# Another order of all steps in a two-layer backbone kernel

## The chip, the cores and the metric

The kernel runs on one core of a Trainium2 chip. The core has five engines that run side by side, each on its own instruction stream: TensorE (PE, matrix products), VectorE (DVE), ScalarE (ACT), GpSimd (POOL) and SyncE (SP), which here issues most of the transfers. The metric is the device time of one execution in microseconds (us); the time of a kernel is the median of its runs. All times below are of the kernel before.

## The reference

A backbone of two layers works on 512 latent tokens of width 1024 and 256 context tokens, all in float32. Each layer has a token mixer and a SwiGLU feed-forward network (FFN, hidden width 2816). Both sit between normalisations whose shift, scale and gate come from a conditioning vector c (called adaLN rows here). Cut to what matters:

```
mod = silu(c) @ ada_w[i] + ada_b[i]            # six rows of 1024: shift, scale, gate, twice
h = rmsnorm(x, norm_g[i, 0]) * (1 + sc) + sh
y = mixer_i(h)                                 # layer 0: windowed attention, layer 1: chunked gMLP
x = x + g * rmsnorm(y, norm_g[i, 1])
f = (silu(h2 @ w_gate) * (h2 @ w_up)) @ w_out  # h2: the same normalisation again, FFN
x = x + g2 * rmsnorm(f, norm_g[i, 3])

gMLP: u, v = split(gelu(h @ w_in + b_in)); v = layernorm(v)
      y = (u * (w_s @ v + b_s)) @ w_o          # w_s mixes the 128 positions of a chunk
```

Layer 0's attention has 16 query heads and 4 key heads, a window of 128 tokens on either side, the context tokens as further keys, and a learned sink logit for each head. Only the latent tokens are an output, and layer 1 does not read the context, so its stream ends as keys and values of layer 0.

## The kernel before, in words

**Arithmetic.** A float32 product is made of three TensorE products: each operand is split into a high part (`high`, line 412, a cast on ACT) and a low part (`low`, line 419, a subtraction on DVE or POOL), and high·high, high·low and low·high are summed in PSUM. The weights are split in the kernel, so all weight data passes through ACT and DVE once before TensorE uses it.

**Weight stream.** The weights come in 88 units of 128x2048 (1 MB). `fetch` issues the transfer of a unit into one of two buffers called `w_raw`; the transfer of unit n waits until the last reader of unit n-2 is done. The split halves are `w_hi` and `w_lo`, four buffers each. A second class of small weights, the `ada_k` chunks of 128x1024, comes through the same SP queue.

**adaLN rows (class Ada).** A row of the second kind is made without TensorE for most of its way: `start` clears an accumulator `acc` on POOL (line 564), eight steps `add_chunk` (line 581, DVE) each add one chunk `ada_k` times a column of silu(c), `fold` (line 595) issues from POOL a transfer that adds the upper 64 partitions of `acc` to the lower ones, `mirror` issues from SP the transfer of the result back to the upper half, `stack` splits it into `acc_st` (ACT line 412, then DVE line 419 on 64 partitions), `total` (line 608) sums it over the partitions on TensorE into `ada_ps`, and `done` (lines 617 to 621) makes the `row`. The names of these steps begin with m and the row's number: m2 is layer 1's third row in its part of the string with "#2" at the end.

**Stages.** In order of time: start and keys/values (0 to 60 us), queries and attention (60 to 230), output projection and the norms behind it (230 to 290), the first FFN's input products (290 to 500), its output product `seven` (500 to 590), norms, the turn and the first part of the gMLP's v (590 to 640), the rest of v, u and the mixing (640 to 700), the gMLP's output product (700 to 755), heads of the second FFN (755 to 790), second FFN to the end (790 to 1108).

**The FFN.** Each of its weight units (22 a layer, numbered n here) is multiplied by a scheme of seven half-size products instead of eight. `diff` (line 1595) makes the sums and differences `T` of quarters of `w_raw`, on DVE (on POOL for the first four units); `part_low` for the first quarter makes `x` (line 419); `product` (line 1635) runs 12 matmuls of 128x256 into a PSUM tile `f`; `keep` (line 1642, ACT), `up2` (line 1646), `up1` (line 1650) and `gate1` (line 1654, all three DVE) combine the products, `silu` and `gates` (line 1665, DVE) end the unit.

**gMLP.** `v_part` (through `mm_a`, line 479) is 12 matmuls of 128x512, `u_part` (lines 2052 to 2054) 24. `vtmp` (line 2020) and `mu` (lines 2028, 2029) belong to the layer norm of v. Behind it, `st` is the split of u times the mixed v (line 2076 makes the factor `uT`), and `work` (line 479) the output product into `y`.

**What sets the order.** All of the work is cut into 3317 steps, each of which issues one or a few instructions on one engine. The program lists the steps with `at(time, step, args)` (line 785), which builds a name from the step and its arguments; the string `ORDER` (lines 41 to 395) holds all names, and a name's place in it is its rank. `run_plan` (line 795) issues the steps by rank:

```
count, rank = {}, {k: i for i, k in enumerate(ORDER)}
...
def run_plan():
    for _, _, key, step, args in sorted(plan, key=lambda e: e[:2]):
        step(*args)
```

No scheduler moves them afterwards. Each engine therefore runs its own instructions in the order of the string, and an instruction whose input is late holds up all that stands behind it on that engine, even if that could run. The same holds for the transfers in the SP queue.

Of the kernel before, what the change touches and what calls it, by code (L numbers as in the profile page):

```python
# [41 lines left out]
warm_0 rope_in x_fetch_5 square_in_5 rstd_in_5 norm_in_5_0 warm_1 norm_in_5_1 warm_2 warm_3 x_fetch_3 square_in_3  # L42
rstd_in_3 norm_in_3_1 dma rope_turn_0 rope_turn_1 x_fetch_4 norm_in_3_0 square_in_4 rstd_in_4 norm_in_4_0 norm_in_4_1
x_fetch_0 turn_in_3_1 x_fetch_1 turn_in_3_0 square_in_0 rstd_in_0 square_in_1 rstd_in_1 turn_in_5_1 turned_in_5_1
norm_in_0_1 warm_4 x_fetch_2 rope_turned_1 square_in_2 norm_in_0_0 turned_in_3_1 turn_in_4_1 rstd_in_2 turn_in_4_0
norm_in_1_0 norm_in_1_1 norm_in_2_0 turned_in_3_0 wfetch_0_0 turn_in_0_0 whigh_0_0 turned_in_0_0 turn_in_0_1
ada0_fetch_0 dma#2 turned_in_4_0 turn_in_5_0 ada0_fetch_1 turned_in_5_0 turn_in_1_0 turned_in_1_0 norm_in_2_1 <lambda>
ada0_rows_0 ada0_rows_out_0 ada0_fetch_2 wlow_0_0 wfetch_0_1 turn_in_2_1 ada0_cols_0 ada0_done_0 modulate0_ctx_0
turn_in_1_1 turn_in_2_0 ada0_rows_1 turned_in_2_0 ada0_fetch_3 modulated_ctx_0 kv_0_5 ada0_rows_out_1 modulate0_0
turned_in_1_1 modulated_high_0 ada0_fetch_4 turned_in_4_1 ada0_cols_1 ada0_done_1 rope_turned_0 kv_0_4 ada0_rows_2 dma#3  # L50
modulated_high_1 modulated_low_0 kv_0_0 modulate0_1 wfetch_1 kv_0_1 ada0_fetch_5 modulate0_ctx_1 m2start ada0_rows_out_2
ada0_cols_2 modulated_low_1 kv_1_0 kv_0_2 kv_1_2 whigh_0_1 wlow_0_1 modulated_ctx_1 ada0_done_2 modulate0_ctx_2 kv_1_1
kv_1_5 ada0_fetch_7 turned_in_2_1 modulated_ctx_2 modulated_high_2 modulate0_2 ada0_rows_3 m2fetch_0 ada0_rows_out_3
ada0_rows_4 ada0_fetch_6 wfetch_2 modulated_low_2 kv_2_2 ada0_cols_3 whigh_1_0 turned_in_0_1 ada0_done_3 modulate0_3
wlow_1_0 kv_0_3 modulated_high_3 kv_1_3 ada0_rows_out_4 modulate0_ctx_3 kv_2_5 m2fetch_1 modulated_low_3 modulated_ctx_3
kv_1_4 ada0_cols_4 ada0_done_4 modulate0_ctx_4 whigh_1_1 kv_2_4 modulated_ctx_4 m2add_0 kv_2_1 kv_3_5 modulated_high_4
ada0_rows_5 ada0_rows_out_5 ada0_rows_7 ada0_rows_out_7 kv_3_4 kv_2_3 kv_2_0 kv_3_0 m2add_1 ada0_cols_5 ada0_done_5
kv_3_2 modulate0_ctx_5 wlow_1_1 modulate0_4 modulated_low_4 dma#4 modulated_high_5 kv_4_5 m2fetch_2 kv_3_3
modulated_ctx_5 modulate0_5 modulated_low_5 kv_4_4 whigh_2_0 ada0_cols_7 ada0_done_7 m2add_2 m2add_3 kv_3_1 kv_4_1
m2fetch_3 ada0_rows_6 ada0_rows_out_6 kv_4_0 kv_5_0 kv_5_1 ada0_cols_6 wlow_2_0 q_first_0_0 whigh_2_1 wlow_2_1 kv_5_4  # L60
q_first_0_1 q_first_0_2 q_first_0_3 kv_4_3 kv_5_3 ada0_done_6 modulated_high_6 modulate0_6 modulated_low_6 kv_6_1 kv_6_0
kv_6_3 modulate0_ctx_6 kv_5_5 modulated_ctx_6 modulate0_7 modulated_high_7 modulated_low_7 kv_7_1 m2add_4 <lambda>#2
kv_7_0 q_first_0_4 q_first_0_5 kv_4_2 kv_5_2 kv_6_2 kv_7_2 kv_7_3 modulate0_ctx_7 modulated_ctx_7 q_first_0_6
q_first_0_7 m2add_5 m2add_6 m2add_7 kv_6_4 kv_7_4 kv_6_5 kv_7_5 wfetch_3 q_first_1_0 q_first_1_1 q_first_1_2 q_first_1_3
table_Exp k_copy_2_0 q_first_1_4 q_first_1_5 v_copy_3 k_copy_2_1 k_rope_2 v_copy_1 v_copy_0 q_first_1_6 k_copy_0_0
k_copy_0_1 k_rope_0 k_add_0 q_rows_0 whigh_3_0 v_copy_2 wlow_3_0_512_1024 whigh_3_1 wlow_3_1_512_1024 q_first_1_7
q_swap_0 k_copy_4_0 k_copy_4_1 wlow_3_0_0_512 k_turn_4_1 k_turn_0_1 k_add_2 wlow_3_1_0_512 q_cos_0 k_turn_0_0 k_turn_2_1
q_rows_1 q_sin_0 q_add_0 k_split_0_1 q_high_0_0 q_low_0_0 q_swap_1 v_copy_4 q_sin_1 k_split_0_0 k_turn_2_0 k_split_2_0
q_cos_1 k_split_4_1 k_turn_4_0 k_split_2_1 q_add_1 v_copy_5 k_split_4_0 q_high_0_1 q_low_0_1 q_high_1_0 q_high_1_1
q_low_1_1 q_low_1_0 wfetch_4 q_step_2_0 q_step_2_1 q_step_2_2 q_step_2_3 q_step_2_4 q_step_2_5 q_step_2_6 q_step_2_7  # L70
m2fold block_0 score_0_0 q_rows_2 score_0_1 bound_0_0 bound_0_1 q_step_3_0 whigh_4_0 wlow_4_0_512_1024 q_step_3_1
q_step_3_2 exp_0_0 m4fetch_0 q_swap_2 q_step_3_3 score_0_3 bound_0_3 score_0_2 bound_0_2 wlow_4_0_0_512 q_cos_2 exp_0_1
q_sin_2 whigh_4_1 exp_0_2 m4start q_step_3_4 q_step_3_5 exp_0_3 sink_0 q_add_2 q_step_3_6 q_step_3_7 q_rows_3
wlow_4_1_0_512 wlow_4_1_512_1024 total_0 normalise_0_0 normalise_0_2 block_1 block_2 block_3 block_4 score_1_0 q_swap_3
score_1_1 bound_1_0 normalise_0_3 q_high_2_0 q_step_4_0 bound_1_1 exp_1_0 exp_1_1 q_low_2_0 m2mirror q_step_4_1
q_step_4_2 score_1_2 m4fetch_1 score_1_3 bound_1_2 exp_1_2 normalise_0_1 bound_1_3 sink_1 m4add_0 q_step_4_3 exp_1_3
q_step_4_4 q_step_4_5 m2fetch_gain total_1 m4add_1 turn_0_0 turn_0_1 turned_0_0 normalise_1_1 m2stack normalise_1_2
score_2_1 bound_2_1 score_2_2 turn_0_2 q_step_4_6 bound_2_2 q_step_4_7 turned_0_2 turn_0_3 block_5 score_2_3 block_6
normalise_1_0 m2total_0_bank_t turned_0_1 score_2_0 turned_0_3 value_0 bound_2_3 exp_2_1 q_step_5_0 score_3_0 exp_2_2
q_rows_4 exp_2_3 normalise_1_3 turn_1_1 turn_1_4 bound_2_0 exp_2_0 sink_2 q_sin_3 block_8 m2done_0 q_step_5_1 score_3_2  # L80
block_7 turned_1_4 m4add_2 bound_3_0 turn_1_0 exp_3_0 turned_1_0 turned_1_1 score_3_1 q_swap_4 total_2 normalise_2_0
q_high_2_1 store_0 normalise_2_1 q_cos_3 turn_1_2 bound_3_2 exp_3_2 turn_1_3 bound_3_1 wfetch_5 q_step_5_2 exp_3_1
q_add_3 q_high_3_0 q_step_5_3 normalise_2_2 normalise_2_3 turned_1_2 turned_1_3 q_cos_4 score_4_0 bound_4_0 q_step_5_4
# [2150 lines left out]
```

## Time and profile before

| what | value |
|---|---|
| runs of the kernel | 1106.84, 1107.83, 1116.1 us; median 1107.83 |
| the profiled execution | 1109.65 us, of which the span from first to last instruction is 1107.9 us |
| busy time in the span | PE 1083.6 us (98%), DVE 941.2 (85%), ACT 602.5 (54%), POOL 264.1 (24%) |
| PE idle in the span | 24.3 us |
| mean granted TensorE clock | 0.995 |
| data moved | 181.25 MB, mean 164 GB/s |

The profile follows one execution. For each engine it gives the busy time by the line of the kernel that issued the instruction and by its operands (`f<-H,w_hi` is a product into `f` from `H` and `w_hi`). A list of waits says for an engine what the instruction that ended an idle time had waited for; the chain of work goes back from a late instruction to what released it, step by step; a table by windows gives busy times, the granted clock (PEclk) and the transfers for stretches of the span. A row of the timeline with `[2.14 <-DMA w_raw<-in_w]` stands for an instruction before which its engine was idle for 2.14 us, until that transfer had landed.

### The profile page before, as it was taken

The numbers are of one execution on the slowest core, as the hardware profiler recorded it, in microseconds if no ns is written. First come the engines' busy times: TensorE is split into PE (matmuls) and PEld (weight loads), VectorE is DVE, ScalarE is ACT, GpSimd is POOL, SyncE is SP. The second block draws the span as 40 slices with busy tenths as digits, with TensorE's granted clock in tenths as the row PEclk, the third lists the DMA queues.
The fourth block names the chain that finished last, engine by engine and source line by source line (L and its number), as shares of the span: only waits on it lengthen the run. The fifth ranks groups of instructions, "written<-read, shape, count | busy, mean of one in ns | idle before, by whom it ended". The sixth has DMA issues, their size and how long they took to land.

```text
span 1107.9 us, 17798 instructions
## 1 busy us (share of the span) xinstructions
PE 1083.6 (98%) x6894; PEld 950.1 (86%) x6894; DVE 941.2 (85%) x1382; ACT 602.5 (54%) x1055; POOL 264.1 (24%) x268
## 2 busy tenths in 40 slices
PE   9999999999999999999999998999999999999997
PEld 5787777778999999998888886878899999998886
DVE  6789998848998999998988687888998888879885
ACT  6356778656544545555665423436555545546662
POOL 2427777526400000002313211006300000003301
PEclk9999999999999999999999998999999999999999
DMA  9745441263255354669943576472143343369821
GB/s 360 280 155 170 144 130 46 80 198 142 77 194 196 128 187 161 195 216 280 219 72 113 196 233 233 137 248 77 38 160 129 131 153 124 125 223 320 165 34 76
DMA packets 50392, 181.25 MB, mean 164 GB/s; under 512 B 5370, under 2 KB 9722, under 8 KB 39172
## 3 DMA queue, kind: packets, MB, share of 16 engines
q1 hardware_dynamic: 42756, 165.44, 43.1%
q0 software_dynamic: 7552, 14.68, 7.7%
q8 instruction: 54, 0.88, 0.3%
q14 instruction: 30, 0.25, 0.1%
HBM read 171.71 MB, written 2.10 MB: 157 GB/s over the span
## 4 chain that ended last, share of the span: by engine, by line
PE 76%; DMA 10%; DVE 8%; issue 3%; ACT 2%; POOL 1%; SPq 1%; DVEq 0%; POOLq 0%; ACTq 0%
PE f L1635 31%; PE y L1819 13%; PE y L479 6%; PE y L1846 6%; DMA w_raw<-in_w 3%; DMA ada_k<-in_ada 2%; PE s_ps L1099 2%; PE pT_ps L1132 2%; PE o_ps L1148 2%; DMA ada_raw<-in_ada 2%; PE q_ps L861 1%; PE v L479 1%; PE fa L473 1%; DVE acc L581 1%; PE fa L471 1%
## 5 line engine op out<-in xcount | busy, mean ns | idle before, releaser
L1635 PE MATMUL f<-H,w_hi 128*128 128x256 f32 x960 | 177.4, 283 | 2.1 <-DVE fc L1646 2.1
L1635 PEld LDWEIGHTS f<-H,w_hi 128*128 128x128 f32 x960 | 149.9, 192 | 2.8 <-DVE fc L1646 2.5
L1635 PE MATMUL f<-H,w_lo 128*128 128x256 f32 x480 | 135.8, 283 | 0.0
L412 ACT CAST w_hi<-w_raw 128x1024 fp32r<-128x1024 f32 x90 | 94.3, 1052 | 60.0 <-DMA w_raw<-in_w 17.0
L1819 PE MATMUL y<-w_hi,s 128*128 128x512 f32 x448 | 120.1, 389 | 0.0
L1635 PE MATMUL f<-S,w_hi 128*128 128x256 f32 x640 | 118.1, 283 | 0.0
L412 ACT CAST w_hi<-T 128x1024 fp32r<-128x1024 f32 x80 | 83.4, 1048 | 58.2 <-PE f L1635 31.7
L1635 PEld LDWEIGHTS f<-S,w_hi 128*128 128x128 f32 x640 | 99.8, 192 | 0.5 <-ACT fc L1642 0.4
L419 DVE TENSOR_TENSOR w_lo<-T,w_hi 128x1024 fp32r<-128x1024 f32 x80 | 97.1, 1217 | 3.5 <-ACT w_hi L412 3.5
L1819 PEld LDWEIGHTS y<-w_hi,s 128*128 128x128 f32 x448 | 84.1, 188 | 17.5
L419 DVE TENSOR_TENSOR w_lo<-w_raw,w_hi 128x1024 fp32r<-128x1024 f32 (+1 forms) x81 | 95.4, 1183 | 4.2 <-ACT w_hi L412 4.2
L595 POOL DMA_DIRECT2D acc<-acc x8 | 6.9, 859 | 366.8 <-DVE acc L581 348.5
L1642 ACT COPY fc<-f 128x256 f32<-128x256 f32 x120 | 44.0, 373 | 92.0 <-PE f L1635 86.8
L1635 PEld LDWEIGHTS f<-H,w_lo 128*128 128x128 f32 x480 | 92.1, 192 | 0.0
L1635 PE MATMUL f<-S,w_lo 128*128 128x256 f32 x320 | 90.7, 283 | 0.0
L581 DVE SCALAR_TENSOR_TENSOR acc<-ada_k,sc,acc 128x1024 f32<-128x1024 f32 x56 | 71.6, 1279 | 13.3 <-DMA ada_k<-in_ada 13.0
L1807 POOL DMA_DIRECT2D t<-in_w x48 | 42.3, 944 | 169.1 <-DMA t<-in_w 95.4
L1819 PE MATMUL y<-w_lo,s 128*128 128x512 f32 x224 | 69.1, 390 | 0.4 <-DVE w_lo L419 0.4
L1635 PE MATMUL f<-H,x 128*128 128x256 f32 x480 | 65.1, 284 | 1.9 <-DVE x L419 1.8
L1126 POOL TENSOR_SCALAR p<-p,st 128x512 f32<-128x512 f32 (+1 forms) x64 | 57.1, 907 | 31.2 <-DVE st L1122 21.8
L1635 PEld LDWEIGHTS f<-H,x 128*128 128x128 f32 x480 | 60.7, 192 | 2.6 <-DVE x L419 2.5
L1110 ACT ACTIVATE p<-s_ps,st 128x512 f32<-128x512 f32 (+1 forms) x64 | 47.3, 740 | 26.4 <-DVE st L1105 24.6
(261 smaller groups left out, 2767.7 us busy)
## 6 DMA issues: line engine op xcount, KB each, us to landing
w_raw<-in_w SPq DMA_DIRECT2D x67, 1024.0 KB, 5.1
ada_k<-in_ada SPq DMA_DIRECT2D x56, 512.0 KB, 6.4
ada_raw<-in_ada SPq DMA_DIRECT2D x12, 1024.0 KB, 5.3
w<-in_w SPq DMA_DIRECT2D x12, 1024.0 KB, 7.0
t<-in_w POOLq DMA_DIRECT2D x48, 256.0 KB, 6.1
ada<-in_ada SPq DMA_DIRECT2D x8, 1024.0 KB, 10.9
t<-in_w SPq DMA_DIRECT2D x8, 1024.0 KB, 14.1
w_raw<-in_w SPq DMA_DIRECT2D x10, 512.0 KB, 5.4
```

Of the source, the lines that this page charges most:

```text
L412: nc.scalar.copy(out=hi, in_=src)
L419: (eng or nc.vector).tensor_tensor(out=v(lo), in0=v(src), in1=v(hi).bitcast(F32), op=ALU.subtract)
L479: nc.tensor.matmul(dst, l, w[:, n * 512:(n + 1) * 512], start=first and i == 0, stop=last and i == 2)
L581: nc.vector.scalar_tensor_tensor(out=self.acc, in0=self.raws.pop(k), scalar=sc[:, k:k + 1], in1=self.acc, op0=ALU.mult, op1=ALU.add)
L1099: nc.tensor.matmul(dst, q, keys, start=i == 0, stop=i == 1)
L1110: nc.scalar.activation(out=p[:, 0:self.n], in_=self.s[j], func=AF.Exp, scale=-1.0, bias=self.st[:, 4 + j:5 + j], accum_out=self.st[:, 8 + ...
L1126: nc.gpsimd.tensor_scalar(out=p, in0=p, scalar1=self.st[:, 12 + j:13 + j], scalar2=1.0, op0=ALU.mult, op1=ALU.mult)
L1635: nc.tensor.matmul(dst, l[:, w], r[:, k, :], start=first and k == 0 and j == 0, stop=k == 3 and j == 2, skip_group_check=True)
L1642: nc.scalar.copy(out=self.c[n][:, i * 256:(i + 1) * 256], in_=self.ps[n, 1 if i == 1 else 0])
L1807: nc.gpsimd.dma_start(out=self.tt[:, p * D + 512 * i:p * D + 512 * (i + 1)], in_=a["w"][F2[self.layer] + 1 + 2 * p + i][:, c:c + 512], acc ...
L1819: nc.tensor.matmul(self.bank7(i, j), st[:, c:c + P], w[:, z * 512:(z + 1) * 512], start=i == 1 and p == 0 and l == 0 and z == 0, stop=p == ...
L1846: nc.tensor.matmul(self.y[t][n], st[:, x + t * P:x + (t + 1) * P], parts[h][w][:, n * 512:(n + 1) * 512], start=v == 0 and h == 0 and i == ...
```

## The change

The string `ORDER` is replaced by another permutation of the same 3317 names. No step is added or taken away, and no instruction, buffer count or engine changes. From the fifth part of the sixth weight unit of the second FFN on (about 790 us in the profile before) the two strings are the same to the end; before that nearly every line differs. Two lines of each, where the gMLP's third adaLN row is made:

```diff
-wlow_47_1 m2fetch_chunk_7 row_in_1 m4fetch_chunk_0 v_part_2_(2,) m2fetch_gain#2 whigh_48_0 wfetch_49 m2add_chunk_7
...
-m2total_512_slot wlow_49_0 m2done_512#2 m4fetch_chunk_5 wlow_49_1 v3var v3rstd u_part_0_0 m2total_0_slot whigh_50_0
...
+m2fetch_chunk_7 m2add_chunk_7 row_in_0 v3add v3gelu v3mean v3gain m4start#2 v_part_0_(2,) v_part_0_(3,) v0add whigh_48_0
...
+v2gelu v2mean m2fetch_gain#2 m2total_512_slot wlow_49_1 whigh_50_0 m4add_chunk_2 m4add_chunk_3 m4add_chunk_4 v2var
```

Behind the last of its eight adds (`m2add_chunk_7`), the string before has one `v_part` and two `u_part` steps ahead of `m2total_512_slot`; the string of the change has three `v_part` and three `u_part` steps there.

**First place: DVE, the gMLP's v.** These are DVE's instructions around the adds of that row (all `acc` rows shown here are adds of that row, x5 standing for five of them; `w_lo`, `w_u` are weight halves and `vtmp` the layer norm). Before:

```order
L581 SCALAR_TENSOR_TENSOR acc<-ada_k,sc,acc 128x1024 x5
L419 TENSOR_TENSOR w_lo<-w_raw,w_hi 128x1024 x2
L581 SCALAR_TENSOR_TENSOR acc<-ada_k,sc,acc 128x1024
L419 TENSOR_TENSOR w_u_6796<-w_raw,w_u_6795 128x1024
L2020 TENSOR_TENSOR vtmp<-v_6596,brow_6774 128x512
L2020 TENSOR_TENSOR vtmp<-v_6597,brow_6774 128x512
L2028 TENSOR_SCALAR mu<-vsum 128x1
L2029 TENSOR_SCALAR mu<-vsum 128x1
L2020 TENSOR_TENSOR vtmp<-v_6670,brow_6774 128x512
L2020 TENSOR_TENSOR vtmp<-v_6671,brow_6774 128x512
L581 SCALAR_TENSOR_TENSOR acc<-ada_k,sc,acc 128x1024
L419 TENSOR_TENSOR w_u_6798<-w_raw,w_u_6797 128x1024
```

The change:

```order
L581 SCALAR_TENSOR_TENSOR acc<-ada_k,sc,acc 128x1024 x3
L419 TENSOR_TENSOR w_lo<-w_raw,w_hi 128x1024 x2
L581 SCALAR_TENSOR_TENSOR acc<-ada_k,sc,acc 128x1024 x4
L419 TENSOR_TENSOR w_u_6816<-w_raw,w_u_6815 128x1024
L419 TENSOR_TENSOR w_u_6818<-w_raw,w_u_6817 128x1024
L581 SCALAR_TENSOR_TENSOR acc<-ada_k,sc,acc 128x1024
L2020 TENSOR_TENSOR vtmp<-v_6742,brow_6774 128x512
L2020 TENSOR_TENSOR vtmp<-v_6743,brow_6774 128x512
```

In the piece before, seven adds are shown and the eighth is the row behind `w_u_6798`, so that four `vtmp` rows stand ahead of the last two adds; in the change all eight adds stand ahead of the first `vtmp`.

**Second place: DVE, the first FFN, two neighbouring weight units.** These rows begin with the last instruction that reads the older `w_raw`, and end with the first that reads the one fetched into the same buffer. Before (the older one is `w_raw_4469`, the newer `w_raw_5072`):

```order
L419 TENSOR_TENSOR w_lo_4992<-w_raw_4469,w_hi_4991 128x1024
L419 TENSOR_TENSOR w_lo_4997<-T_4815,w_hi_4996 128x1024
L1595 TENSOR_TENSOR T_5074<-w_raw_4875 128x512 x2
L1665 TENSOR_TENSOR act4_5089<-fc_4699,silu_4969 128x2x256
L1595 TENSOR_TENSOR T_5074<-T_5074,w_raw_4875 128x512
L1665 TENSOR_TENSOR act4_5089<-fc_4773,silu_4878 128x2x256
L419 TENSOR_TENSOR w_lo_5097<-T_4841,w_hi_5096 128x1024
L1654 TENSOR_TENSOR f2_5046<-f2_5046,fc_4927 128x256
L1595 TENSOR_TENSOR T_5115<-w_raw_5072 128x512
```

The change, without its first two rows (the older one is `w_raw_4863`, last read by a `T` right ahead of these rows, the newer `w_raw_5156`):

```order
L419 TENSOR_TENSOR w_lo_4983<-w_raw_4980,w_hi_4982 128x1024
L1665 TENSOR_TENSOR act4_5055<-fc_4682,silu_4902 128x2x256
L1595 TENSOR_TENSOR T_5001<-T_5001,w_raw_4980 128x512
L1654 TENSOR_TENSOR f2_4985<-f2_4985,fc_4900 128x256
L1665 TENSOR_TENSOR act4_5055<-fc_4771,silu_4953 128x2x256
L1654 TENSOR_TENSOR f2_5084<-f2_5084,fc_5049 128x256
L581 SCALAR_TENSOR_TENSOR acc_4704<-ada_k_4999,sc_69,acc_4704 128x1024
L419 TENSOR_TENSOR w_lo_5144<-T_4923,w_hi_5143 128x1024
L1595 TENSOR_TENSOR T_5001<-w_raw_4980,T_5001 128x512
L1665 TENSOR_TENSOR act4_5055<-fc_4900,silu_5113 128x2x256
L419 TENSOR_TENSOR w_lo_5153<-T_5001,w_hi_5152 128x1024
L419 TENSOR_TENSOR x0_5161<-w_raw_5156,x0_5161 128x512
```

Between the last read of the older unit and the first read of the newer one DVE has 8 instructions before and 13 in the change: the 11 shown ahead of the last row and, ahead of those, one `up2` (`fc_4900<-f0_4885`, line 1646) and one `up1` (`fc_4900<-f1_4937`, line 1650).

**Third place: DVE, the gMLP's output product.** `st` is what its matmuls read, `acc` the adds of the next row. Before:

```order
L581 SCALAR_TENSOR_TENSOR acc<-ada_k,sc,acc 128x1024 x2
L619 SCALAR_TENSOR_TENSOR row<-ada_ps,row 128x512
L419 TENSOR_TENSOR w_lo<-w_raw,w_hi 128x1024
L581 SCALAR_TENSOR_TENSOR acc<-ada_k,sc,acc 128x1024
L419 TENSOR_TENSOR st<-uT,st 128x512
L581 SCALAR_TENSOR_TENSOR acc<-ada_k,sc,acc 128x1024
L419 TENSOR_TENSOR st<-uT,st 128x512
```

The change:

```order
L619 SCALAR_TENSOR_TENSOR row<-ada_ps,row 128x512
L419 TENSOR_TENSOR st<-uT,st 128x512
L2071 TENSOR_TENSOR m<-mix,bs 128x512
L419 TENSOR_TENSOR st<-uT,st 128x512
L419 TENSOR_TENSOR w_lo<-w_raw,w_hi 128x1024
L581 SCALAR_TENSOR_TENSOR acc<-ada_k,sc,acc 128x1024
L2076 TENSOR_TENSOR uT<-uT,m 128x512
L581 SCALAR_TENSOR_TENSOR acc<-ada_k,sc,acc 128x1024
```

Two of the `st` rows have moved from behind the adds to ahead of them; the other `st` rows stand elsewhere in both.

More of the change, by code (lines that the diff above doesn't have):

```diff
@@ L47 @@
[L47 to L71, printed above, removed]
@@ new lines @@
+f1up2_20 f1part_low_21_3 f1fetch7_11_0_raw f1product_21_5 f1fetch7_11_1_big f1keep_21_0 f1fetch7_12_0_big f1product_20_4
+f1keep_21_1 f1silu_20_0 m5stack#2 f1product_21_6 f1silu_20_1 f1gates_20 f1set_split_0 f1product_21_2 f1keep_21_2
+whigh_77_0 f1take7_0 f1product_21_3 f1gate1_21 wlow_77_0 whigh_77_1 f1take7_1 wlow_77_1 f1product_21_7 f1fetch7_12_1_raw
+f1up1_21 m5total_0_slot#2 f1plain7_0_2 gains f1up2_21 m5done_0#2 f1product_21_4 m5total_512_slot#2 f1save7_v0_0
+f1silu_21_0 m5done_512#2 f1plain7_0_3 f1fetch7_12_0 f1silu_21_1 f1fetch7_12_1 f1fetch7_21_0 f1gates_21 f1fetch7_21_1
```

676 lines of the change are left out of this document (348 added, 328 removed).

## The prediction

> **What bounds the kernel now.** I read the page first, then the windows by stage, then TensorE's waits, and last the chain and the timeline at each wait. The page says that TensorE is the bound:
>
> ```profile
> span 1107.9 us, 17798 instructions
> PE 1083.6 (98%) x6894; PEld 950.1 (86%) x6894; DVE 941.2 (85%) x1382; ACT 602.5 (54%) x1055; POOL 264.1 (24%) x268
> ```
>
> PE is idle for 1107.9 - 1083.6 = 24.3 us, and another order of the same instructions can take away no more than that, and what a slower clock costs. The windows, cut at the stages, say where it is idle (columns: window, its length, busy us and count of PE, PEld, DVE, ACT, POOL, then PEclk, DMA share, GB/s):
>
> ```profile
> 0.00:60.00 60.00, 56.22 (x380) 38.31 (x381) 42.00 (x92) 30.36 (x52) 22.54 (x31) 1.00 0.83 317
> 60.00:230.00 170.00, 166.90 (x1075) 132.62 (x1074) 148.54 (x293) 116.91 (x264) 103.09 (x113) 1.00 0.38 122
> ...
> 290.00:500.00 210.00, 206.05 (x1683) 203.53 (x1682) 199.19 (x271) 109.89 (x189) 2.99 (x4) 1.00 0.53 179
> 500.00:590.00 90.00, 90.00 (x404) 74.69 (x403) 78.48 (x96) 54.67 (x74) 21.25 (x24) 1.00 0.74 187
> ...
> 640.00:700.00 60.00, 56.25 (x254) 46.62 (x253) 45.46 (x56) 20.94 (x30) 7.83 (x8) 0.94 0.65 208
> 700.00:755.00 55.00, 53.36 (x250) 43.85 (x249) 46.38 (x57) 26.16 (x40) 4.87 (x4) 1.00 0.56 186
> ...
> 790.00:1107.90 317.90, 311.04 (x2161) 291.21 (x2159) 267.17 (x365) 164.11 (x270) 25.07 (x29) 0.99 0.47 144
> ```
>
> Length less PE gives the idle: start 3.8, attention 3.1, first FFN 4.0, gMLP 3.75, its output product 1.6, the part behind 790 us 6.9; the heads ahead of that have a wait of 1.2, below; the three stages in between (230 to 290, 500 to 590, 590 to 640) have none. So 17.4 us lie where the order changes; the last 6.9 us, like all behind 790 us, belong to steps whose order stays. PEclk is below 1.00 before that only in the gMLP. The waits name the causes (columns: engine, waiting instruction, releaser: us in total, times, longest):
>
> ```profile
> PE ada_ps L608 <- DVE acc_st L419: 3.7, 1, 3.7
> PE f L1635 <- DVE fc L1646: 2.1, 2, 1.4
> PE warm L684 <- DVE idle L681: 1.8, 1, 1.8
> PE f L1635 <- DVE x L419: 1.8, 2, 1.5
> PE s_ps L1099 <- ACT p L1110: 1.6, 4, 0.7
> PE y L479 <- DVE st L419: 1.2, 1, 1.2
> PE fa L473 <- DVE H L419: 1.2, 1, 1.2
> ...
> PE y L479 <- DVE row L619: 0.4, 1, 0.4
> ```
>
> No wait but the first is long. TensorE takes its work from DVE nearly everywhere, and DVE, 85% busy, is the engine to watch.
>
> **The change, part by part.** It removes and adds no instruction, so every term is a wait that goes, stays or is new.
>
> *gMLP, the third adaLN row.* The chain of waits from this row's last add to its total (start, us, what):
>
> ```profile
> 654.11 1.28 DVE acc L581
> ...
> 655.75 10.30 DMA acc<-acc
> ...
> 666.06 1.92 DMA acc<-acc
> ...
> 670.09 1.23 DVE acc_st L419
> ...
> 671.37 0.80 PE ada_ps L608
> ```
>
> From the end of the add (655.39) to the total (671.37) it takes 16.0 us, 12.2 of them the fold and the mirror. TensorE stops at the total because it has too little to do meanwhile. One matmul of 128x512 comes every 0.227 us: 13 steps lie between the first and the third of these rows, 2.95 us:
>
> ```profile
> 664.29 0.39 PE L2053 MATMUL u<-H,w_hi 128*128 128x512 f32 x1
> ...
> 667.24 0.39 PE L2054 MATMUL u<-H,w_lo 128*128 128x512 f32 x1
> 671.37 0.80 PE L608 MATMUL ada_ps<-acc_st,ones 128*128 128x512 f32 x1 [3.75 <-DVE acc_st L419]
> 671.96 0.63 PE L2052 MATMUL u<-H,w_u 128*128 128x512 f32 x1
> 672.39 0.63 PE L2053 MATMUL u<-H,w_u 128*128 128x512 f32 x1
> ```
>
> The string before has one `v_part` (12 matmuls, 2.7 us) and two `u_part` (24 each, 5.45 us) behind the last add: 13.6 us. The change has three and three: 3 x 2.7 + 3 x 5.45 = 24.5 us, 8.5 more than the 16.0 needed. The add itself is not later on DVE: the first place of the change shows that four `vtmp` rows left its front. On SP the mirror is now behind the weight transfer of unit 49, whose buffer was last read ahead of the eighth add, so that it does not hold the queue; on POOL the fold stands behind the clearing of an `acc`, as before. **The 3.7 us go.** With them goes a slower stretch: behind the wait, matmuls come every 0.43 us (671.96 to 672.39), until about 677:
>
> ```profile
> 671.00:674.00 3.00, 2.63 (x6) 2.15 (x7) 2.97 (x8) 1.33 (x3) 0.00 (x0) 0.50 0.90 355
> 674.00:677.00 3.00, 3.00 (x8) 2.29 (x8) 1.21 (x5) 2.97 (x5) 0.84 (x1) 0.52 0.68 246
> 677.00:682.00 5.00, 5.00 (x23) 4.13 (x22) 4.93 (x7) 0.17 (x2) 2.08 (x2) 1.00 0.16 26
> ```
>
> The granted clock is 0.50 there, and 1.00 again behind it. In the 5.04 us from 671.96 to 677 there is room for 11.8 matmuls at 0.427 us, which at 0.227 us take 2.7: 2.3 us lost. Waits of up to 1.8 us lower the clock of no other window ahead of 790 us, so with the wait these 2.3 us go too. **Together -6.0 us**; bounds 0 (the chain gets later by 8.5 us after all) and -6.4.
>
> The Trainium skill ("TensorE: Matmul & The Clock Gate", Part 1: The HAM clock gate) speaks against a part of this: the clock falls to half only after at least one idle window of about 3.4 us, and that window runs freely, so that it depends on where in it a stall falls. An estimate from that page: a stall of 3.75 us holds a whole window for (3.75 - 3.41) / 3.41, one in ten, of the phases; the trace's one long wait did meet it, and no second trace here shows how often it does. By that rule most runs of the kernel before would not have lost the 2.3 us, the gain in the median would be 3.7, and the time 2.3 us longer than the one worked out here, 1100.5. I keep the row.
>
> *First FFN, 290 to 500 us.* PE loses 4.0 us here, in the four waits on `fc` and `x`. DVE is busy 199.2 of 210 us, so its order can only be bettered where it waits itself. It does, for weights:
>
> ```profile
> 444.15 7.76 DMA w_raw<-in_w
> ```
>
> ```profile
> 444.05 1.22 DVE L419 TENSOR_TENSOR w_lo<-T,w_hi 128x1024 fp32r<-128x1024 f32 x1
> ...
> 449.45 0.42 DVE L1654 TENSOR_TENSOR f<-f,fc 128x256 f32<-128x256 f32 x1
> 452.01 0.69 DVE L1595 TENSOR_TENSOR T<-w_raw 128x512 f32<-128x512 f32 x1 [2.14 <-DMA w_raw<-in_w]
> ...
> 454.42 0.42 DVE L1646 TENSOR_TENSOR fc<-f,fc 128x256 f32<-128x256 f32 x1
> ```
>
> The buffer comes free at 444.1 and the transfer takes 7.76 us, but DVE has only 5.8 us of other work (444.05 to 449.87) before the first instruction that reads it. Behind that instruction stands the `up2` that TensorE waits for: 1.4 us. In the change the same distance is 13 instructions (second place): three `w_lo` of 1.22, one `acc` of 1.28, five of 0.69 (like the `T` above) and four of 0.42 (like the `f` and the `up2`) make 10.1 us, by those rows and these:
>
> ```profile
> L419 DVE TENSOR_TENSOR w_lo<-T,w_hi 128x1024 fp32r<-128x1024 f32 x80 | 97.1, 1217 | 3.5 <-ACT w_hi L412 3.5
> L581 DVE SCALAR_TENSOR_TENSOR acc<-ada_k,sc,acc 128x1024 f32<-128x1024 f32 x56 | 71.6, 1279 | 13.3 <-DMA ada_k<-in_ada 13.0
> ```
>
> Instructions overlap by some 0.07 us (444.05 + 1.22 runs into the next), 0.9 over 13 of them: 9.2 us are left, over 7.76, so that wait goes. I counted the same lead at each unit on the two strings in TensorE's work, a product at 12 x 206.05 / 1683 = 1.5 us, from the last reader of a buffer to the first product of the unit fetched into it. Before, six units have 7.2 to 13.0 us; in the change two have 10.0 and 10.1 and the rest 14.4 or more. Six short leads gave four waits of 1.0 us in the mean; two should give one or two. **-2.6 us**, with 1.4 left; bounds -4.0 (none left) and +2 (a `up2` of the change that has some 11 us of DVE work behind 8.6 us of lead comes 2.4 us late, and the waits stay).
>
> *gMLP's output product, 700 to 755 us.* `st` waits behind an add on DVE that waits for its chunk:
>
> ```profile
> 726.81 1.28 DVE L581 SCALAR_TENSOR_TENSOR acc<-ada_k,sc,acc 128x1024 f32<-128x1024 f32 x1 [1.92 <-DMA ada_k<-in_ada]
> 728.01 0.68 DVE L419 TENSOR_TENSOR st<-uT,st 128x512 fp32r<-128x512 f32 x1
> ```
>
> In the third place of the change two `st` stand ahead of the adds, and the 1.2 us go; so do the 0.4 us for `row`, which stands right behind its total's stage. **-1.6 us**; bounds -1.6 and +1.9 (an add's wait of 1.92 in front of another instruction).
>
> *Heads, 755 to 790.* Of the two `H` low parts that the heads wait for, one stands earlier and one where it stood: half of 1.2, **-0.6 us**, bounds -1.2 and 0.
>
> *Start and attention.* New orders throughout. Where ACT before stood at the cast of a weight just fetched, it stands so again in the change at another unit (fetch and cast adjacent before the first exponentials):
>
> ```profile
> 139.31 1.06 ACT L412 CAST w_hi<-w_raw 128x1024 fp32r<-128x1024 f32 x1 [1.08 <-DMA w_raw<-in_w]
> ```
>
> One such stop goes and one comes. **0**; bounds -5.1 (3.8 + 3.1 less the 1.8 of the warm-up, which waits for the first memory write and not for an order) and +3 (three stops of 1.08).
>
> *First FFN's output product, 500 to 590.* No idle now, so it can only lose. By the strings nine of its 28 products stand in the change directly behind the step that makes their low weight part, where before each had 2.7 us or more of matmuls between. DVE has 90 - 78.5 = 11.5 us free there, which hides most of it. I take one `w_lo` of 1.22 not hidden: **+1.2 us**; bounds 0 and 9 x 1.22 = 11.
>
> Sum: -6.0 - 2.6 - 1.6 - 0.6 + 0 + 1.2 = -9.6. The profiled execution, 1109.65 us (span 1107.9 and 1.75 around it), becomes 1100.05. It is 1.8 us over the median, 1107.83, which becomes **1098.2 us**.
>
> **The rivals.** *Nearly all waits before 790 us vanish.* Idle 17.4, less 1.8 of the warm-up, plus 2.3 of clock: -17.9, 1089.9 us. For it: all are of one kind, a few us of bad luck in an order that the transfers' real durations overtook. Against: the start is bound by transfers (DMA share 0.83). Chance 0.24. *Only the gMLP's term is real*, and the small waits come back at other units, since DVE is as full as before: 1107.83 - 6.0 = 1101.8. Chance 0.24. *DVE is late in the first FFN's output product*: each of the nine products waits for its whole `w_lo`, +11.0, which decides as soon as DVE comes out of the FFN with over 11.5 us of backlog; with the gMLP's -6.0 that makes 1112.8, slower than before. Against: the stage shows not one wait now. Chance 0.09. *No net change*: the gMLP's chain is held up on SP or POOL by what it was moved past, and gains equal losses, 1107.8; chance 0.05.
>
> **How the numbers follow.** The forecast has 0.38, with its own range 1094 to 1102. 1% of the time before, about what a measurement tells from no change, is 11.1 us: the bounds are 1096.8 and 1118.9. Faster: the first rival 0.24, and some 0.4 of the forecast, 0.15, with 0.01 of the second, together 0.40. Slower by over 1%: the third rival with a little more on top, 0.05. Same: 0.55. The range runs from 1087, a little under the first rival (start and attention may give more), to 1110, which leaves out the third rival; outside lie some 0.15.
>
> **What would show it.** Right: no wait of `ada_ps` over 1 us and PEclk 1.00 between 640 and 700 us; at most two waits of TensorE on `fc` or `x` before 500; `y` waiting for no `st`; PE busy near 1081 us and its idle near 17. Wrong: a window between 500 and 590 us with PE under 99%, more than 4 us of waits on `fc` or `x`, or attention with over 5 us of idle; then the chain will name `w_lo` or `w_hi`. If the gMLP's wait is still there, the 16 us of the chain grew, and the fold or the mirror will have started late.

## The result and the profile after

The changed kernel takes 1097.8 us in the median of 4 runs (1097.12 to 1098.59), the kernel before in the same comparison 1108.11 us: ratio 0.9892, 95% interval 0.9845 to 0.9939. A second comparison gave 1097.46 against 1110.29 us, ratio 0.988 (0.9842 to 0.9918). The prediction was 1098.2 us. The sum came out right; one of its terms was 3.4 us off, and the five others turned out 0.6 to 1.7 us better than predicted.

The profiled execution took 1098.59 us. From the page of the changed kernel:

```profile
span 1096.8 us, 17794 instructions
...
PE 1077.8 (98%) x6894; PEld 948.3 (86%) x6894; DVE 939.1 (86%) x1382; ACT 601.0 (55%) x1055; POOL 263.1 (24%) x268
```

PE's idle time went from 24.3 to 19.0 us and its busy time fell by 5.8 us, though it does the same matmuls. Part of that is the half clock of the gMLP, which is gone; the rest comes from how a busy time is made: the end of a matmul is modelled, so a short stop between two matmuls is partly counted as busy. The windows, cut as before:

```profile
0.00:60.00 60.00, 55.18 (x382) 38.73 (x382) 42.45 (x93) 30.80 (x52) 20.89 (x31) 1.00 0.83 317
60.00:230.00 170.00, 167.47 (x1087) 133.56 (x1086) 146.89 (x292) 117.20 (x266) 103.16 (x115) 1.00 0.40 124
...
290.00:500.00 210.00, 208.97 (x1700) 206.40 (x1699) 202.00 (x275) 107.80 (x188) 5.26 (x6) 1.00 0.56 187
500.00:590.00 90.00, 86.39 (x378) 70.24 (x377) 74.37 (x91) 53.28 (x72) 21.27 (x24) 1.00 0.69 161
...
640.00:700.00 60.00, 60.00 (x291) 50.58 (x290) 51.18 (x63) 23.63 (x33) 7.79 (x8) 1.00 0.69 226
700.00:755.00 55.00, 55.00 (x260) 45.96 (x259) 45.22 (x57) 29.25 (x52) 9.17 (x8) 1.00 0.49 162
755.00:790.00 35.00, 35.00 (x215) 31.30 (x214) 33.10 (x46) 19.10 (x32) 19.61 (x14) 1.00 0.24 80
```

The gMLP, its output product and the heads have no idle time left, and the first FFN has 1.0 us instead of 4.0. The FFN's output product, which had none, has 3.6 us, and the start has 4.8 us instead of 3.8. TensorE's longest waits, less the warm-up's 1.8:

```profile
PE xT L697 <- DVE r L446: 1.6, 1, 1.6
PE y L1819 <- ACT s L412: 1.3, 1, 1.3
PE s_ps L1099 <- DVE klo L419: 1.2, 1, 1.2
PE y L1819 <- DVE s L419: 1.2, 1, 1.2
PE xT L697 <- DVE xin L676: 1.2, 2, 0.7
PE y L1819 <- DVE w_lo L419: 1.1, 1, 1.1
PE s_ps L1099 <- ACT p L1110: 1.0, 2, 0.7
PE f L1635 <- DVE fc L1646: 0.5, 1, 0.5
PE f L1635 <- ACT fc L1642: 0.5, 1, 0.5
```

The waits of `xT` lie in the start. All three waits of `y` at line 1819 lie in the first FFN's output product. The waits that cost over 1 us before, of `ada_ps` (line 608) on `acc_st` and those on `x`, `st` and `H`, are no longer in the list; of the two on `fc`, the one for ACT lies at 486 us and the one for DVE at 811 us, in the second FFN.

Because idle time understates a stop, the account by stages uses the distances from each matmul's start to the next, less the usual distance of its shape (0.227 us for 128x512, 0.119 for 128x256), summed by stage of the timeline:

| stage | lost before | lost after | moved | predicted |
|---|---|---|---|---|
| start and attention, to 230 us | 17.2 | 15.5 | -1.7 | 0 |
| first FFN, 290 to 500 | 7.6 | 3.8 | -3.8 | -2.6 |
| its output product, 500 to 600 | -0.1 | 4.5 | +4.6 | +1.2 |
| gMLP with its half clock, 600 to 700 | 6.8 | 0.2 | -6.6 | -6.0 |
| its output product, 700 to 760 | 2.5 | 0.1 | -2.4 | -1.6 |
| heads, 760 to 800 | 1.7 | 0.2 | -1.6 | -0.6 |
| the rest | 2.5 | 2.9 | +0.4 | 0 |
| sum | 38.3 | 27.2 | -11.1 | -9.6 |

The last matmul starts 11.1 us sooner (1101.00 to 1089.94 us), which is this sum; the medians differ by 10.3.

**The new stop.** TensorE, ACT, SP and DVE around 533 us in the changed kernel, in four timelines and one piece of the chain:

```profile
534.81 0.73 PE L1819 MATMUL y<-w_hi,s 128*128 128x512 f32 x2 [1.32 <-ACT s L412]
536.67 0.74 PE L1819 MATMUL y<-w_lo,s 128*128 128x512 f32 x2 [1.13 <-DVE w_lo L419]
541.35 0.96 PE L1819 MATMUL y<-w_hi,s 128*128 128x512 f32 x3 [1.17 <-DVE s L419]
```

```profile
532.24 1.99 ACT L412 CAST w_hi<-t 128x1024 fp32r<-128x1024 f32 x2 [8.02 <-DMA t<-in_w]
534.14 1.13 ACT L412 CAST s<-act 128x512 fp32r<-128x512 f32 x2
```

```profile
495.33 1.47 SPq L409 DMA_DIRECT2D t<-in_w  x3
516.97 0.37 SPq L409 DMA_DIRECT2D w<-in_w  x1
517.38 0.51 SPq L409 DMA_DIRECT2D t<-in_w  x1
```

```profile
515.72 1.22 DVE L1801 TENSOR_TENSOR t<-w,w 128x1024 f32<-128x1024 f32 x1
```

```profile
517.38 14.76 DMA t<-in_w
```

ACT stood for 8.0 us at the cast of a weight quarter that landed at 532.1, and the casts of `s` that TensorE needed stood behind it. The transfer took 14.8 us, but it was issued late: three transfers into `t` were issued at 495 us, the fourth at 517.4, right behind one into `w`. That one had to wait 19.8 us, by SP's own list of waits, until DVE (line 1801, done at 516.9) had read its buffer, and SP's queue waited with it. Before, all four went out one after the other at 503.5 us and the `w` behind them:

```profile
503.48 2.42 SPq L409 DMA_DIRECT2D t<-in_w  x4
510.36 0.99 SPq L409 DMA_DIRECT2D w<-in_w  x2
```

### The profile page after: what moved, and what is told of

Read it like the earlier page. It is cut to its first block, busy times and chain, and to the rows that moved or that the text cites. A ratio compares the mean times of both kernels' runs of the same rounds, so it can differ in the third digit from the quotient of the medians.

```text
span 1096.8 us, 17794 instructions
## 1 busy us (share of the span) xinstructions
PE 1077.8 (98%) x6894; PEld 948.3 (86%) x6894; DVE 939.1 (86%) x1382; ACT 601.0 (55%) x1055; POOL 263.1 (24%) x268
## 4 chain that ended last, share of the span: by engine, by line
PE 89%; DVE 5%; DMA 3%; issue 1%; ACT 1%; SPq 0%; DVEq 0%; POOLq 0%; POOL 0%; ACTq 0%
PE f L1635 36%; PE y L1819 12%; PE y L479 7%; PE y L1846 6%; PE v L479 4%; PE s_ps L1099 2%; PE pT_ps L1132 2%; PE o_ps L1148 2%; PE q_ps L861 1%; DMA t<-in_w 1%; PE fa L471 1%; PE fa L473 1%; PE fa L472 1%; PE u L2054 1%; PE u L2053 1%; PE u L2052 1%
## 5 line engine op out<-in xcount | busy, mean ns | idle before, releaser
L1642 ACT COPY fc<-f 128x256 f32<-128x256 f32 x120 | 43.6, 372 | 84.2 <-PE f L1635 75.6
L1126 POOL TENSOR_SCALAR p<-p,st 128x512 f32<-128x512 f32 (+1 forms) x64 | 59.8, 948 | 27.5 <-DVE st L1122 14.5
L1635 PEld LDWEIGHTS f<-S,w_lo 128*128 128x128 f32 x320 | 61.4, 192 | 0.0
```

Of the source, the lines that this page charges most:

```text
L1126: nc.gpsimd.tensor_scalar(out=p, in0=p, scalar1=self.st[:, 12 + j:13 + j], scalar2=1.0, op0=ALU.mult, op1=ALU.mult)
L1635: nc.tensor.matmul(dst, l[:, w], r[:, k, :], start=first and k == 0 and j == 0, stop=k == 3 and j == 2, skip_group_check=True)
L1642: nc.scalar.copy(out=self.c[n][:, i * 256:(i + 1) * 256], in_=self.ps[n, 1 if i == 1 else 0])
```

## The experiments

The strings before and after hold the same set of names up to the places 236, 293, 981, 1753, 2006, 2101, 2327 and 2537. So any stretch between two of these places can be taken from the one or the other. In the edits below, B is the string before and A the changed one. Each comparison ran with the kernel before on the same chip; the first four kernels, the next four and the last four shared one chip each. The ratio is estimated from all runs with its interval, and is not exactly the quotient of the two medians.

| kernel | median, runs | before | ratio (95% interval) |
|---|---|---|---|
| b_gmlp | 1100.74, 5 | 1109.52 | 0.9905 (0.9873 to 0.9937) |
| b_ffn | 1102.65, 9 | 1109.52 | 0.9956 (0.9934 to 0.9978) |
| b_seven | 1116.98, 10 | 1109.52 | 1.006 (1.004 to 1.0081) |
| b_attn | 1107.35, 10 | 1109.52 | 0.9973 (0.9953 to 0.9993) |
| a_fix | 1096.16, 4 | 1108.9 | 0.9874 (0.9847 to 0.9901) |
| b_break | 1114.26, 10 | 1108.9 | 1.003 (1.0002 to 1.0059) |
| b_add | 1108.81, 10 | 1108.9 | 1.0003 (0.9979 to 1.0026) |
| a_seven | 1094.85, 4 | 1108.9 | 0.9854 (0.9823 to 0.9885) |
| b_total | 1107.91, 10 | 1110.29 | 0.9969 (0.9945 to 0.9993) |
| b_lead | 1105.58, 10 | 1110.29 | 0.9964 (0.994 to 0.9988) |
| a_best | 1098.54, 4 | 1110.29 | 0.9888 (0.985 to 0.9925) |
| after_again | 1097.46, 4 | 1110.29 | 0.988 (0.9842 to 0.9918) |

### One stretch of the change at a time

```diff
-ORDER = B
+ORDER = B[:2101] + A[2101:2327] + B[2327:]   # b_gmlp
+ORDER = B[:981] + A[981:1753] + B[1753:]     # b_ffn
+ORDER = B[:1753] + A[1753:2006] + B[2006:]   # b_seven
+ORDER = A[:293] + A[293:981] + B[981:]       # b_attn
```

> The order of before with one stretch of steps from the change: the turn of the gMLP, its v, u, mixing and output product. Theory (each stage has its own waits, and they add up): the 3.9 us stop at the third row's total, the half clock behind it (2.3) and the stops on st and row (2.35 by the distances between matmuls) go, 8.6 to 8.9 us less than before, about 1099.3 us, with PEclk 1.00 throughout. Rival (what a stage gains is given back at the next one, since DVE is as full as before): not more than 6 us less, with a new stop of over 1 us at the heads.

The gMLP's windows of b_gmlp (640 to 700 and 700 to 755 us):

```profile
640.00:700.00 60.00, 60.00 (x290) 50.59 (x289) 52.21 (x65) 23.63 (x33) 7.79 (x8) 1.00 0.70 231
700.00:755.00 55.00, 53.50 (x250) 44.05 (x249) 44.70 (x57) 28.73 (x51) 9.74 (x8) 1.00 0.47 156
```

From the first u matmul to the second FFN its trace gains 8.0 us, and the median is 8.8 us lower. The stops on `st`, `row` and the total are gone; a new one of 1.1 us on `tmp` (line 1339) stands at the seam, where two orders meet that were not made for each other. The theory holds, with a small part of the rival.

> The order of before with the stretch of the output projection and nearly all of the first FFN's input products from the change. Theory: the stops on fc and x go, 3 to 4 us less, about 1104.5 us, and the FFN's output product stays without a stop, as in before. Rival (the change's stop of about 4 us in that output product comes from a backlog on DVE that the FFN's order leaves behind): a stop of over 2 us appears between 500 and 590 us, and the time is not under 1107 us.

The window of the output product in b_ffn has PE busy for 90.00 of 90 us, and no wait on DVE's `fc` or `x` is left. So the FFN's order does not leave a backlog behind: the theory holds. From the end of attention to the FFN's last product the trace gains 3.5 us. The median is 6.9 us lower (2.4 to 7.3 by the interval of the ratio). The whole trace gains 7.0 us, and 3.1 of them come behind the last product of u, where the order is that of before; why is not settled.

> The order of before with the stretch of the first FFN's end and its output product from the change. Theory (the stop there comes from the order of the transfers in that stretch itself): 4 to 5 us of stops on s and w_lo as in the change, 4 to 5 us more than before, about 1112.6 us. Rival (backlog from the FFN's order): no stop over 1 us there, 1108 us.

The stops of `y` on `s` and `w_lo` appear in b_seven at 545 to 552 us, 3.5 us in all by the distances, and SP shows the same picture 12 us later than in the changed kernel:

```profile
528.81 0.37 SPq L409 DMA_DIRECT2D w<-in_w  x1
529.22 0.59 SPq L409 DMA_DIRECT2D t<-in_w  x1
```

The stop belongs to this stretch's own order. The 7.5 us of the median (4.4 to 9.0 by the interval of the ratio) are more than these stops; 2.5 us of further stops at 493 to 500 us, where the two orders meet, are in the trace as well.

> The order of before with the three first stretches (start, keys and values, attention) from the change. Theory: 1.5 to 2 us less, about 1106.4 us; the start is a little longer, attention shorter. Rival: within 1 us of before, the differences there being chance of one profiled execution.

2.5 us sooner at the end of attention, in the trace; 2.1 of them were lost again in the FFN, where a stop of 2.5 us at 452 us and a half clock behind it appeared in an order that had not been changed. The median's gain of 2.2 us agrees with the theory, though its interval nearly reaches no change.

### The transfer that stood in the wrong place

```diff
 ORDER of the change, a_fix
-f0fetch7_12_1 f0a7_low_1_2 f0fetch7_22_0_raw ... f0w7_high_2_0 f0fetch7_21_1
+f0fetch7_12_1 f0a7_low_1_2 f0fetch7_21_1 f0fetch7_22_0_raw ... f0w7_high_2_0
 ORDER of before, b_break
-f0fetch7_21_0 ... f0fetch7_21_1 ... f0fetch7_22_0_raw
+f0fetch7_21_0 ... f0fetch7_22_0_raw f0fetch7_21_1
```

> The order of the change with one step moved: the transfer of the second half of quarter 21 of the first FFN's output weights is issued ahead of the first half of quarter 22 on SP, instead of behind it. Theory (the 4 us of stops in that output product come from this one transfer, which stood in SP's queue behind one that waited 21 us for a buffer): it is issued some 20 us sooner, ACT's wait of 8.0 us at the casts of that quarter goes, and so do the three stops of TensorE; 3.5 to 4.5 us less than the change, about 1093.8 us. Rival (backlog on DVE, nine products directly behind their low part): the stops stay within 1 us of what they were, 1097.8 us.

SP of a_fix issues all four together, from 494.6 us on; the fourth had gone out at 517.4:

```profile
494.58 2.31 SPq L409 DMA_DIRECT2D t<-in_w  x4
516.22 0.37 SPq L409 DMA_DIRECT2D w<-in_w  x1
```

```profile
522.44 1.05 ACT L412 CAST w_hi<-t 128x1024 fp32r<-128x1024 f32 x1 [3.44 <-DMA t<-in_w]
```

Of the three stops one of 1.1 us is left (525.5 us, on `s`), behind a wait of ACT of 3.4 us for another transfer into `t`. From the FFN's last input product to its last output product the trace takes 89.0 us instead of 91.6, so 2.6 us are gained, and 1.9 of the 4.5 us stay lost. The median is only 1.3 to 1.6 us lower than the changed kernel's in its two comparisons (1097.8 and 1097.46); these comparisons are not that of a_fix, and the intervals of the ratios overlap, so the medians alone do not tell the two apart. The mechanism is as the theory has it, and the size is under the 3.5 to 4.5 us that it expected.

> The order of before with the same step moved the other way: the second half of quarter 21 behind the first half of quarter 22 on SP. Theory: ACT waits several us more at its cast, and TensorE stops in the first FFN's output product, where before it never did; 2 to 4 us more than before. Rival: nothing over 1 us, since the transfer is hidden anyway.

TensorE stops where it had never stopped, for the transfer that SP issued behind the other:

```profile
532.50 1.01 PE L1819 MATMUL y<-w_hi,s 128*128 128x512 f32 x2 [2.08 <-ACT w_hi L412]
533.75 1.22 PE L1819 MATMUL y<-w_lo,s 128*128 128x512 f32 x2 [0.25 <-DVE w_lo L419]
```

The stage takes 5.0 us more (89.3 instead of 84.2 us from the FFN's last input product to its last output product): 2.9 us in the two stops shown, a half clock behind them, and smaller ones. The median is 5.4 us higher (0.2 to 6.5 by the interval of the ratio). One transfer's place in SP's queue makes the stop here and takes most of it away in a_fix.

```diff
-ORDER = A
+ORDER = A[:1753] + B[1753:2006] + A[2006:]   # a_seven
```

> The order of the change with the stretch of the first FFN's end and its output product taken from before. Theory (stages add up): that stretch alone cost 7.5 us in the order of before, so some 4 to 7 us less than the change, about 1092 us, with no stop over 0.5 us between 500 and 590 us. Rival (that stretch only cost so much behind the FFN of before): not under 1096.5 us.

No stop between 500 and 590 us, and 1094.85 us: 2.6 to 3.0 us less than the changed kernel in its two comparisons, its four runs (1093.48 to 1095.21) all under the changed kernel's eight. These comparisons, too, are others, and the intervals of the ratios overlap; but in the traces the last matmul starts 3.4 us sooner. That is the lowest median of this study. It is less than the theory's 4 to 7: the same stretch costs 7.5 us in the order of before, 2.5 of them at the seam, and about 3 in that of the change, so the stages do not simply add up.

### The gMLP's chain

```diff
-v_part_3_(3,) wlow_47_1 m2fetch_chunk_7 ... m2add_chunk_7       b_add: ORDER of before
+v_part_3_(3,) m2fetch_chunk_7 ... m2add_chunk_7 wlow_47_1
-m2total_512_slot wlow_49_0 ... v3rstd u_part_0_0 m2total_0_slot  b_total: ORDER of before
+u_part_0_0 m2total_512_slot wlow_49_0 ... v3rstd m2total_0_slot
```

> The order of before with one DVE instruction moved: the eighth add of the gMLP's third row is run ahead of a weight's low part (1.2 us) and not behind it. Theory: the chain to that row's total starts 1.1 us sooner and the stop of 3.9 us becomes 2.7 us or so; and since a stop that short has never lowered the clock in these traces, the half clock behind it goes as well, 3.4 us less than before. Rival (the clock falls behind any stop over 2 us): 1.1 us less.

From its list of waits:

```profile
PE ada_ps L608 <- DVE acc_st L419: 2.1, 1, 2.1
PE y L479 <- DVE st L419: 2.1, 1, 2.1
```

The stop at the total shrank to 2.1 us of idle and the clock stayed at 1.00 behind it, as the theory expected, and u ends 3.0 us sooner. But the wait on `st` grew from 1.2 to 2.1 us, and this time the half clock came behind that one: six matmuls 0.427 us apart. `v` added 0.8 us, and 1.9 us were back by the end of the output product. From start to start the stop at the total is 2.47 us and the one on `st` 2.45, so the expectation's premise that so short a stop never lowers the clock does not hold. The median shows nothing (0.9979 to 1.0026). Of the expected 3.4 us about 1 remains in the trace: a miss.

> The order of before with one TensorE step moved: a u_part of 24 matmuls (5.45 us) ahead of the third row's first total, not behind it; no other engine's instructions move. Theory: the stop of 3.9 us and the half clock behind it go, 5 to 6.5 us less by the end of u. Of the eighth add run sooner, the stretch up to the end of u gained 3 us, but 1.9 of them were given back at st and v behind it; so here too 1 to 2 us come back in the output product, where DVE is unchanged, and 4 us remain at the end. Rival (all of it stays): 6 us remain at the end. Rival (all is given back, as in the median of the other run): within 1.5 us of before.

All was given back, and at once. DVE and TensorE in b_total:

```profile
673.07 1.22 DVE L419 TENSOR_TENSOR acc_st<-acc,acc_st 64x1024 fp32r<-64x1024 f32 x1 [3.26 <-ACT acc_st L412]
...
678.90 0.15 DVE L446 TENSOR_SCALAR rv<-var 128x1 f32<-128x1 f32 x1 [1.78 <-ACT junk L439]
678.97 1.22 DVE L419 TENSOR_TENSOR w_lo<-w_raw,w_hi 128x1024 fp32r<-128x1024 f32 x1
```

```profile
PE u L2054 <- DVE w_lo L419: 3.7, 1, 3.7
```

The total no longer waits, but the next product does, for as long: its `w_lo` stands in DVE's queue behind `acc_st`, which waits for the same fold and mirror, and behind parts of the layer norm, the last of which waits 1.78 us for ACT. More matmuls ahead of the total were not enough. In the changed kernel DVE does `acc_st` without any wait and long before the total:

```profile
661.19 1.22 DVE L419 TENSOR_TENSOR acc_st<-acc,acc_st 64x1024 fp32r<-64x1024 f32 x1
```

```profile
672.13 0.39 PE L608 MATMUL ada_ps<-acc_st,ones 128*128 128x512 f32 x1
```

So the change seems to start the chain early enough for every engine that it passes through; this is read from the traces, since b_gmlp moves the whole stretch and no run moves the chain alone. The interval of b_total's median (0.9945 to 0.9993) allows a small gain; its trace shows none in this stage.

### The first FFN's order on DVE

```diff
 ORDER of before, b_lead
-f0gate1_16 f0diff_19_1 f0part_low_18_0 f0diff_19_3 ... f0up2_16 ... f0up1_17 f0gate1_17 f0up2_17
+f0gate1_16 f0part_low_18_0 ... f0up2_16 ... f0up1_17 f0gate1_17 f0up2_17 f0diff_19_1 f0diff_19_3
```

> The order of before with two steps moved, on DVE alone: the two first differences from the weight unit that arrives at 452 us stand behind the two up2, the up1 and the gate1 that TensorE waits for, not ahead of them. Theory (TensorE waits there only because these four stand in DVE's queue behind an instruction that waits for a transfer): DVE has 4 us of other work for the 2.1 us that it waited, and TensorE's stop of 1.6 us at 455 us goes or falls under 0.4 us; the other stops of the FFN stay. In the median that is 0.15%, less than such runs tell apart. Rival (DVE is behind by its sum of work, not by its order): the stop moves on by a few us and keeps its size.

DVE in b_lead, at the place where it had waited 2.14 us for the weights:

```profile
454.52 0.42 DVE L1654 TENSOR_TENSOR f<-f,fc 128x256 f32<-128x256 f32 x1
455.60 0.42 DVE L1646 TENSOR_TENSOR fc<-f,fc 128x256 f32<-128x256 f32 x1 [0.65 <-PE f L1635]
455.94 1.28 DVE L1595 TENSOR_TENSOR T<-w_raw 128x512 f32<-128x512 f32 x2
```

The two differences no longer wait, the `up2` waits for TensorE instead of TensorE for it, and no stop of TensorE is left within 15 us; the next one in the FFN (474 us, 0.43 us) is small. The theory holds: it is the place in the queue, not DVE's sum of work. The median is 4.7 us lower (1.3 to 6.7 by the interval of the ratio), more than this stop is worth; the trace, of one of the slower runs (1109.0 us), does not show why.

### A further edit, and the changed kernel again

```diff
 ORDER of a_seven, a_best
-m1total_512_slot m1total_0_slot ... m1done_0 m1done_512 ... f0product_21_6
+f0product_21_6 m1total_512_slot m1total_0_slot m1done_0 m1done_512
```

> The order of the change with the first FFN's end and output product from before, and in that stretch the two totals of layer 0's second adaLN row moved behind one more product of 12 matmuls, with the two steps that use them. Theory: the stops of 0.9, 0.5 and 0.4 us at these totals, which stood in the trace of the same order without this last edit, go, 1 to 1.8 us less than its 1094.9 us, about 1093.4 us. Rival: the stops only move to the product's own wait behind them, 1094.9 us.

The theory failed. The stops moved to the product's own wait, as the rival says, but the wait was 4.1 us (on ACT's `fc`) and the median came to 1098.54 us, more than the rival's 1094.9.

```profile
484.90 0.62 ACT L412 CAST acc_st<-acc 128x512 fp32r<-128x512 f32 x1 [3.15 <-PE f L1635]
...
488.48 0.37 ACT L1642 COPY fc<-f 128x256 f32<-128x256 f32 x1 [1.96 <-DVE act L1665]
```

That `fc` waited for DVE's `act`, which stands behind two `acc_st` and a `row`. The totals had filled a gap that was there for another reason. Why the gap itself grew from some 1.8 to 4.1 us is not settled.

> The changed kernel itself, unedited, on the same chip and in the same rounds as the other three. Both theories: 1097 to 1099 us, and a spread from the shortest to the longest run of 3 us or less, where the kernel before spread over 15 us.

The runs took 1097.02 to 1098.62 us, as expected.

## Why the prediction was right, point by point

**The bound and the list of places** were right for what was gained: it came where TensorE had stopped before 790 us. The order differs a little longer than was said, up to about 820 us of the trace before, but TensorE had no wait between 790 and 820. Two stops are new: the 4.6 us of the output product, in a stage that had none, and one of 0.7 us from start to start at 811 us (the wait on DVE's `fc`). The signs that were named were seen: no wait of `ada_ps` at line 608, PEclk 1.00 in the gMLP, one wait of 0.5 us on `fc` before 500 us, and `y` waiting for no `st`. PE's idle time came to 19.0 us and not 17, and its busy time to 1077.8 and not 1081. The sign for "wrong" was there as well: PE at 86.39 of 90 us, 96%, between 500 and 590 us.

**gMLP, -6.0; measured -6.6.** The wait and the half clock behind it both went. The reason given was incomplete: enough matmuls behind the last add do not suffice if DVE's own part of the chain still blocks the next weight. b_total had 13.6 + 5.45 = 19.1 us of them, 3 us more than the 16.0 of the chain, and gained nothing up to the end of u. The change had moved DVE's part too, because its eight adds come sooner; the order of DVE that was shown says so, but the sum did not use it.

**The estimate from the Trainium skill against the row.** By the page "TensorE: Matmul & The Clock Gate" (Part 1: The HAM clock gate) it was estimated that most runs of before would not meet the half clock. The traces do not agree. Six traces run the gMLP in the order of before without an edit there, and all six have the half clock behind this stop. In the 14 traces there are eight stops of 3.6 us or more (start to start), and behind each of them, at once or after a few matmuls, those of 128x512 came every 0.427 us. The row was the better guide.

**First FFN, -2.6; measured -3.8.** The mechanism was right and the size was under it: two of the weight units were expected to keep a wait, and none did. In the trace of before DVE waited four times for `w_raw` (1.71, 0.56, 1.62 and 2.14 us), in the changed kernel not once. The count of leads was too coarse to tell 10 us from too little.

**Its output product, +1.2; measured +4.6.** This is the step that failed. It counted which products stand directly behind their `w_lo`, and priced one of them. In a_fix, where the nine stand as they stood, no wait on a `w_lo` is left in this stage, so none of them makes a stop by itself. The prediction did not read SP's queue, where a transfer had moved behind one that waits for a buffer: 8.0 us of ACT's time, three stops. The rival that named this stage had the wrong engine for its cause, and 4.5 instead of 11 us.

**gMLP's output product, -1.6, and heads, -0.6; measured -2.4 and -1.6.** Here the waits went entirely. Both terms were too small since they were read from idle time: the wait of 1.2 us on `st` was a distance of 1.64 us, 1.4 over the usual one. For the heads, halving the 1.2 us was the larger error, since neither `H` was waited for.

**Start and attention, 0; measured -1.7.** This is within the bounds. For the start it is not clear of chance: in the eight traces that run it in the order of before, the end of the keys and values lies from 67.6 to 69.7 us (69.4 in the trace that the prediction read), in the six with that of the change from 68.6 to 69.1. For attention it is: from there to its last product `o_ps` the eight take 161.1 to 163.1 us, the six 159.7 to 160.4. The reason for the 0 failed there: ACT's stop of 1.08 us at the cast of a weight went, but none came at another unit; the changed trace has no wait of ACT for `w_raw` between 60 and 232 us. Which of the other moves in attention helped was not tested.

The errors were +3.4 in one term, +0.4 in the rest, and -0.6, -1.2, -0.8, -1.0 and -1.7 in the others. They sum to -1.5 on the traces, the medians moved 0.8 us less than the traces, and the kernel before took 0.3 us longer in this comparison than in the runs that the prediction started from; so the time agrees to 0.4 us, by more luck than the single terms had.

## What to carry to other kernels

When a change reorders steps, read the transfers' own queue as closely as the engines': a transfer that waits for its buffer holds all that stand behind it, and their readers with them. A wait in the middle of a chain is only removed when every engine that the chain passes through is early; in b_total, where it was moved on one engine alone, it came back at the next product. Short stops are better read as distances from start to start than as idle time.

## What the runs showed that was not expected

**The spread went with the waits.** The kernel before took 1104.12 to 1119.2 us over 19 runs of one comparison, the changed one 1097.02 to 1098.62 over its 8 runs. The traces show one place of it. From the first to the last product of the first FFN, six traces with the order of before took 221.25, 221.37, 222.04, 223.36, 223.59 and 225.41 us; three with that of the change took 218.32, 218.31 and 218.32. In the one DVE waits for transfers of `w_raw`, the longest of which took 7.4 us in one trace and 10.8 in another; in the other it waits for none. That these waits make the spread is a reading of the traces. b_ffn, where DVE has no such wait either, spread over 4.8 us in 9 runs, the kernel before on the same chip over 8.7 in 25, so they are at most a part of it.

**The clock fell behind shorter stops, too.** In the 14 traces, by distances from start to start behind 60 us: all 8 stops of 3.6 us or more were followed by the lower clock, so were 8 of 13 stops between 2.1 and 2.8 us, and of those between 1.5 and 1.9 us only one, the second of a pair in after_again (532 and 534 us); the same pair in the changed kernel's first trace did not. A group of shorter stops did it too: 0.9, 0.5 and 0.4 us close together in a_seven (485 to 488 us), with a granted clock of 0.54 in the 3 us behind them. The Trainium skill ("TensorE: Matmul & The Clock Gate", Part 1: The HAM clock gate) names at least one idle window of about 3.4 us; the measurements differ from that. Two windows of b_ffn show how it looks, a stop of 4.8 us that ends in the second half of the first:

```profile
665.00:670.00 5.00, 2.10 (x7) 1.70 (x8) 3.35 (x6) 1.85 (x2) 0.00 (x0) 0.87 0.99 338
670.00:675.00 5.00, 5.00 (x19) 4.05 (x18) 3.21 (x7) 3.67 (x7) 1.46 (x1) 0.78 0.53 184
```

Three matmuls still came at full speed there and some eight at 0.427 us behind them. So a stop of 2.5 us from start to start may cost 2.2 us, like that at the total in b_add, or about 3.9, like that on `st` in the same trace, and that may be one more source of the spread.
